# A fused eight-layer stack on one core: state-space inputs, small transfers and parameter work in another order

## The chip, the cores and the metric

The kernel runs on one core of a Trainium2 chip. The metric is the device time of one execution in microseconds (us); less is better. Five engines work side by side, each through its own stream in program order: PE (TensorE, matrix products), DVE (VectorE), ACT (ScalarE), POOL (GpSimd) and SP (SyncE, which only starts transfers here). ACT starts transfers too, in its own stream.

## What is computed

One sequence of 256 positions and width 2048 goes through two layers of a first block (a pooling mixer, dilated attention, each followed by a squared-ReLU MLP) and one layer of a second block, all in fp32. The change touches the mixer of the second block. Cut to it:

```
hn = rmsnorm(h, attn_norm_w);  proj = hn @ w_in            # 2048 -> 1024 + 512 + 256 + 64
u, c_q, c_kv, k_pe = split(proj)
# state-space group (S5): 64 groups of 16 inputs and 64 complex states
abar = exp(lam * dt);  zbar = (abar - 1) / lam;  bbar = zbar * b
s[t] = abar * s[t-1] + bbar @ u[t]                         # scan over 256 steps
y    = gelu(Re(c @ s) + d * u);  y_ssm = y * sigmoid(y @ w_glu + b_glu)
# latent attention (MLA), 8 heads, rotary on 64 of 192 dims, causal softmax
q = rmsnorm(c_q) @ w_uq;  k_nope, v = rmsnorm(c_kv) @ w_ukv
y_mla = softmax(mask(q k^T)) v
h = h + concat(rmsnorm(y_ssm), rmsnorm(y_mla)) @ w_out
```

A gated convolution MLP and a last norm follow.

## The kernel before

Activations lie as channel tiles of 128 channels by 256 positions. Every weight is streamed from HBM once, in units of 128 x 1024 elements (shorter ones in places). SP loads a unit (`raw`, `load_next`), ACT casts it to its high part (`hi`, L148), DVE subtracts for the low part (`lo`, L156), and PE makes three products, hi x hi, hi x lo and lo x hi (`mm3`, L206 to L208 in the second mixer, L211, L212 and L214 elsewhere). `take` keeps the high parts three units ahead of PE and the low parts three (two in the second mixer). A `slab` is a block of output columns over all input tiles. When its last product is issued, a generator (`on_done`) evacuates the accumulator and does what follows.

All other work is written as generators. After each weight unit `tick` runs one segment of every live generator (`step`) and takes one item of a background list (`pump`). So the code order, and with it each engine's stream, is set by how many `yield`s lie between two segments: one `yield` is one unit of PE work later.

**Parameters.** `ssm_params` (L888 to L1077) computes from the state-space parameters all that the mixer needs and stores it in HBM: `d_tab` (tables of powers of abar for the scan), `d_b` and `d_c` (128 x 512 and 128 x 768 blocks for each of eight groups of eight). It runs in the background of the first MLP, one segment for each unit. Its parts in order: loads of the parameters through ACT's stream (L897 to L905), an exponential (L907), a copy into `nat` (L908), three transposes on PE (L912), angle, magnitude and z on 128 x 32 tiles on DVE, complex products `cmul` (L923; six such tiny DVE operations each, all recorded on L921), the table on POOL (L988, L992), then for each of eight q: masked c (`cm`, POOL), b products (`pd` L1023, `bm` L1028, POOL), their transposes on PE (L1033, L1040), the pe/wl products (POOL) and final products (L1061).

**Second mixer.** `plan_mix2` lists the order of the weights, `run_mix2` uses them. w_in's first slab (four u tiles of 128 channels) starts before the norm's sums are ready (`raw`). Then come the c_q slab, the c_kv and k_pe slab, and the heads: projections of latents in two halves a = 0 and 1, and attention for two to four heads under them (`scores`, `soft`, `flip`, `attend`, `put`). The u tiles 4 and 5 are a slab under half a = 0, and 6 and 7 one under half a = 1. Then w_out's lower half on the MLA outputs (eight slabs), the GLU product (four slabs), and w_out's upper half on the state-space outputs.

**State-space steps.** For each of eight groups q, `ssm_step` does two half steps. The even one: products `bu` (L1184) from `us` and `qb`, and for the group two before (LAG = 2) `ssm_out`, products `y` (L1219). The odd one: `ssm_in` (DVE and POOL rotate bu), `ssm_mid` (scans and rotation back). `ssm_pace` lets a step go every second unit or so. Before a step, `u_done` (L1290) normalises a u tile (`ut`, POOL), stores it (`d_u`, L1301), and `load_u` loads it back as four transfers in another layout (`us`, L1157). `load_b`, `load_rec` and `load_c` (two transfers of 128 x 512, one of 128 x 512, two of 128 x 768) fetch that group's tables. After `y`, `gelu` copies y out of the accumulator (`yt`, L1227, ACT), stores it (`d_y`, L1228), loads it back as u (L1233) and applies Gelu (L1239). All of these transfers stand in ACT's stream. Statistics of the norms are sums on PE with a vector of ones (L334) over squares that POOL or ACT makes (`Sq`, L320 to L322).

A step asks for its input with these lines (before):

```
if not odd:
    if q < 8:
        if q not in us:
            if q in u_in:
                load_u(q)
            return False
        ssm_bu(q)
        if q < 7:
            load_b(q + 1)
```

Of the kernel before, what the change touches and what calls it, by code (L numbers as in the profile page):

```python
# [62 lines left out]
class Net:  # L63
# [824 lines left out]
    def ssm_params(self, sp):  # L888
# [53 lines left out]
        ni, zr, zi = a1[:, 1, :], z[:, 0, :], z[:, 1, :]  # L942
        tt(den, lr, lr, ALU.mult)
# [6 lines left out]
        tt(zr, zr, den, ALU.mult)  # L950
        tt(zi, ni, lr, ALU.mult)
# [20 lines left out]
        for n, a in ((2, a1), (1, a2), (0, a3)):  # L972
            cmul(e1, z, a)
            V.tensor_copy(zt[:, :, :, n], e1)
        for n, a in enumerate((a1, a2, a3, a4)):
            V.tensor_copy(at[:, :, :, n], a)
# [32 lines left out]
        for q in range(8):  # L1009
# [5 lines left out]
            wide = [P, 4, CH, 16]  # L1015
            for n in range(2):
                for a in range(2):
                    G.tensor_scalar(cm[:, n, a, :], cn[n][:, q, :], msk[:, 2 * n + a:2 * n + a + 1], None, op0=ALU.mult)
                prod = [sp.tile([P, 512], F32, tag=f"tmp{x}", name=f"pd{x}")[:, 0:256] for x in range(2)]
                prod = [x.rearrange("p (s l h) -> p s l h", s=4, l=CH) for x in prod]  # L1020
# [10 lines left out]
            pc = self.aux([P, 2, P])  # L1031
            for n in range(2):
                nc.tensor.transpose(pc[:, n, :], cm[:, n].rearrange("p a c -> p (a c)"), self.ident)  # L1033
            for n in range(2):
                nc.scalar.copy(wl[n][:, :, 0, :], pc[:, n, :].rearrange("p (s r) -> p s r", s=4))
            yield
            for n in range(2):
# [4 lines left out]
                yield  # L1042
# [36 lines left out]
    def plan_mix2(self):  # L1079
# [25 lines left out]
        for s in range(8):  # L1105
            self.want_slab(wo, 1024, 8, s * 256, nn=2)
# [669 lines left out]
```

## Time and profile before

| | |
|---|---|
| median of 3 runs | 3405.5 us (3404.15 to 3406.73) |
| profiled execution, its own time | 3404.18 us |
| span of its trace | 3402.4 us |
| mean granted PE clock | 0.977 of full |
| PE busy | 3277.6 us, 96% |
| DVE busy | 2142.9 us, 63% |
| ACT busy | 1606.5 us, 47% |
| POOL busy | 1233.2 us, 36% |

The table is read as follows. The span is the profiled execution from its first to its last instruction; busy is the time in which an engine worked on any instruction. The granted clock is a mean over the span: 1.00 is 2.4 GHz and 0.50 is 1.2 GHz. Lines L... are lines of the kernel before, unless a sentence says that they are of the changed one.

### The profile page before, as it was taken

The numbers are of one execution on the slowest core, as the hardware profiler recorded it, in microseconds if no ns is written. First come the engines' busy times: TensorE is split into PE (matmuls) and PEld (weight loads), VectorE is DVE, ScalarE is ACT, GpSimd is POOL, SyncE is SP. The second block draws the span as 40 slices with busy tenths as digits, with TensorE's granted clock in tenths as the row PEclk, the third lists the DMA queues.
The fourth block names the chain that finished last, engine by engine and source line by source line (L and its number), as shares of the span: only waits on it lengthen the run. The fifth ranks groups of instructions, "written<-read, shape, count | busy, mean of one in ns | idle before, by whom it ended". The sixth has DMA issues, their size and how long they took to land.

```text
span 3402.4 us, 49683 instructions
## 1 busy us (share of the span) xinstructions
PE 3277.6 (96%) x19452; PEld 2892.3 (85%) x19452; DVE 2142.9 (63%) x2748; ACT 1606.5 (47%) x2477; POOL 1233.2 (36%) x1371
## 2 busy tenths in 40 slices
PE   8998999999999999999999999996889999999999
PEld 7896888888898899988888888886879888888887
DVE  5777566665676545576565656674545686687585
ACT  4654444444554444465444444562346544444344
POOL 6454866662252000073121112454447332142141
PEclk9999999999999999999999999997789999999999
DMA  6555666666555554545555555544535555555554
GB/s 220 178 189 147 201 200 211 205 220 195 174 193 170 165 179 156 173 160 175 186 179 193 192 189 180 182 153 133 168 103 162 172 177 197 179 190 198 179 181 172
DMA packets 452165, 610.56 MB, mean 179 GB/s; under 512 B 56036, under 2 KB 262746, under 8 KB 451930
## 3 DMA queue, kind: packets, MB, share of 16 engines
q1 hardware_dynamic: 423914, 588.93, 53.0%
q10 hardware_dynamic: 27872, 17.87, 1.9%
q8 instruction: 152, 2.49, 0.3%
q14 instruction: 83, 0.68, 0.1%
q0 software_dynamic: 144, 0.59, 0.1%
HBM read 590.54 MB, written 16.78 MB: 178 GB/s over the span
## 4 chain that ended last, share of the span: by engine, by line
PE 80%; POOL 10%; DVE 4%; ACT 2%; issue 2%; DMA 1%; ACTq 1%; SPq 0%; POOLq 0%; DVEq 0%
PE acc L214 37%; PE acc L212 20%; PE acc L277 4%; PE acc L276 4%; PE acc L275 4%; PE acc L211 2%; PE acc L206 2%; PE acc L207 2%; PE acc L208 1%; DVE lo L156 1%; POOL w L629 1%; POOL X L441 1%; POOL tmp L988 1%; POOL hid L301 1%; PE y L1219 1%
## 5 line engine op out<-in xcount | busy, mean ns | idle before, releaser
L156 DVE TENSOR_TENSOR lo<-raw,hi 128x1024 fp32r<-128x1024 f32 x1094 | 1459.9, 1360 | 600.2 <-ACT hi L148 598.9
L214 PE MATMUL acc<-xs,hi 128*128 128x512 f32 x4020 | 1429.7, 397 | 9.5 <-POOL xs L445 9.4
L148 ACT CAST hi<-raw 128x1024 fp32r<-128x1024 f32 x1094 | 1118.9, 1045 | 574.5 <-PE acc L214 374.8
L212 PE MATMUL acc<-xs,lo 128*128 128x256 f32 x4288 | 1166.3, 282 | 8.6 <-DVE lo L156 8.6
L214 PEld LDWEIGHTS acc<-xs,hi 128*128 128x128 f32 x4020 | 761.1, 189 | 176.5 <-POOL xs L445 11.3
L212 PEld LDWEIGHTS acc<-xs,lo 128*128 128x128 f32 x4288 | 814.0, 190 | 32.8 <-DVE lo L156 10.1
L214 PE MATMUL acc<-hid,hi 128*128 128x512 f32 x1920 | 684.3, 396 | 0.0
L212 PE MATMUL acc<-hid,lo 128*128 128x256 f32 x2048 | 557.4, 282 | 3.4 <-DVE lo L156 3.4
L685 POOL TENSOR_TENSOR X<-X,c 128x256 f32<-128x256 f32 x152 | 134.3, 895 | 879.7 <-DVE X L683 566.1
L214 PEld LDWEIGHTS acc<-hid,hi 128*128 128x128 f32 x1920 | 361.5, 188 | 80.6
L212 PEld LDWEIGHTS acc<-hid,lo 128*128 128x128 f32 x2048 | 385.2, 188 | 16.4 <-DVE lo L156 4.0
L301 POOL TENSOR_TENSOR hid<-t,hid 128x256 fp32r<-128x256 f32 x128 | 147.1, 1173 | 447.6 <-ACT hid L300 445.1
L291 ACT COPY c<-acc 128x256 f32<-128x256 f32 x264 | 97.4, 373 | 305.4 <-PE acc L214 291.9
L206 PE MATMUL acc<-xs,hi 128*128 128x256 f32 (+1 forms) x768 | 223.6, 291 | 11.9 <-ACT t L287 5.6
L207 PE MATMUL acc<-xs,hi 128*128 128x256 f32 (+1 forms) x768 | 221.2, 288 | 1.1 <-DVE xs L447 0.6
L208 PE MATMUL acc<-xs,lo 128*128 128x256 f32 (+1 forms) x768 | 219.7, 286 | 0.6 <-DVE lo L156 0.6
L1624 POOL TENSOR_TENSOR a<-t,r 128x256 f32<-128x256 f32 x88 | 66.8, 761 | 369.9 <-DVE t L292 347.1
L292 DVE TENSOR_TENSOR t<-acc,c 128x256 f32<-128x256 f32 x208 | 87.5, 423 | 164.8 <-ACT c L291 162.3
L679 ACT COPY c<-acc 128x256 f32<-128x256 f32 x160 | 59.4, 373 | 219.2 <-PE acc L214 189.8
L206 PEld LDWEIGHTS acc<-xs,hi 128*128 128x128 f32 x768 | 149.7, 195 | 13.4 <-ACT t L287 6.2
L207 PEld LDWEIGHTS acc<-xs,hi 128*128 128x128 f32 x768 | 149.9, 195 | 1.9 <-DVE xs L447 0.8
L208 PEld LDWEIGHTS acc<-xs,lo 128*128 128x128 f32 x768 | 150.0, 195 | 1.0 <-DVE lo L156 1.0
(324 smaller groups left out, 4333.1 us busy)
## 6 DMA issues: line engine op xcount, KB each, us to landing
raw<-in_mlp_w_up_dram SPq DMA_DIRECT2D x128, 1024.0 KB
raw<-in_mlp_w_down_dram SPq DMA_DIRECT2D x128, 1024.0 KB
raw<-in_ffn_w_up_dram SPq DMA_DIRECT2D x176, 512.0 KB
raw<-in_attn_w_qkv_dram SPq DMA_DIRECT2D x96, 512.0 KB
raw<-in_ffn_w_down_dram SPq DMA_DIRECT2D x44, 1024.0 KB
raw<-in_attn_w_qkv_dram SPq DMA_DIRECT2D x24, 1024.0 KB
raw<-in_pool_w_in_dram SPq DMA_DIRECT2D x16, 1024.0 KB
raw<-in_pool_w_out_dram SPq DMA_DIRECT2D x16, 1024.0 KB
```

Source lines behind the costliest of these rows:

```text
L148: self.nc.scalar.copy(to(hi), src)
L156: self.nc.vector.tensor_tensor(out=to(lo), in0=src, in1=to(hi).bitcast(F32), op=ALU.subtract)
L206: nc.tensor.matmul(acc[:, 0:n], lhsT=hi, rhs=x[:, 0:n], start=first, stop=False)
L207: nc.tensor.matmul(acc[:, 0:n], lhsT=hi, rhs=x[:, n:2 * n], start=False, stop=False)
L208: nc.tensor.matmul(acc[:, 0:n], lhsT=lo, rhs=x[:, 0:n], start=False, stop=last)
L212: nc.tensor.matmul(acc[:, T:2 * T], lhsT=lo, rhs=x[:, 0:T], start=False, stop=False)
L214: nc.tensor.matmul(acc, lhsT=hi, rhs=x, start=False, stop=last)
L275: nc.tensor.matmul(a, lhsT=xh, rhs=hi[:, k, :], start=first and (t == 0 or not one), stop=False)
L276: nc.tensor.matmul(a, lhsT=xh, rhs=lo[:, k, :], start=False, stop=False)
L277: nc.tensor.matmul(a, lhsT=xl, rhs=hi[:, k, :], start=False, stop=last and (t == 1 or not one))
L301: (eng or nc.vector).tensor_tensor(out=xs[:, T:2 * T], in0=src, in1=xs[:, 0:T].bitcast(F32), op=ALU.subtract)
L685: (nc.vector if norm is not None and j >= KD - 2 else nc.gpsimd).tensor_tensor(out=x, in0=x, in1=c, op=ALU.add)
```

## The change

**Parameters.** Two segments more before the exponential and the copy into `nat`, three more before the transposes. The angle and z work is in five segments in place of two. One `cmul` runs in each segment; before, there were three, two, four, four and five (with the copies) in each. The table on POOL begins 18 units later (unit 29 of that stage against 11). In the loop over q, masked c and its transposes come first; the transposes of `bm` come one unit after its products for n = 1 and two for n = 0 (three before); the store into `d_b` comes two units later; two segments lie before the last products.

**Second mixer.** u tiles 4 and 5 are a slab directly behind the first one, so ahead of the c_q slab; u tiles 6 and 7 stay under half a = 1. `load_u` is now a generator in three segments, started from the even half step before: product on POOL, store, then the four loads. `load_rec(q)` comes right behind `bu` of q; `load_b` and `load_c` go to the odd half step. `gelu` stores y one segment behind the copy. Two of the eight w_out slabs on the MLA outputs go behind the GLU slabs; for that, the GLU output lies in tiles of its own instead of in `xs`.

```diff
         yield
+        yield
         nc.scalar.activation(ldt, ldt, AF.Exp)
         V.tensor_copy(nat[:, 2, :].rearrange("s (a p) -> s a p", a=2), ldt.to_broadcast([NS, 2, 64]))
-        yield
+        for _ in range(3):
+            yield
         ps = self.aux([P, 3, NS])
...
-        cmul(e2, e1, e1)
-        cmul(e3, e2, e1)
-        cmul(ep[:, 0], e2, e2)
-        yield
-        for n in range(1, NK):
-            cmul(ep[:, n], ep[:, n - 1], ep[:, n - 1])
-            if n % 2 == 0:
-                yield
-        cmul(a2, a1, a1)
-        cmul(a3, a2, a1)
-        cmul(a4, a2, a2)
-        yield
+        powers = [(e2, e1, e1), (e3, e2, e1), (ep[:, 0], e2, e2)]
+        powers += [(ep[:, n], ep[:, n - 1], ep[:, n - 1]) for n in range(1, NK)]
+        powers += [(a2, a1, a1), (a3, a2, a1), (a4, a2, a2)]
+        for w_ in powers:
+            cmul(*w_)
+            yield
...
                 yield
-            pc = self.aux([P, 2, P])
-            for n in range(2):
-                nc.tensor.transpose(pc[:, n, :], cm[:, n].rearrange("p a c -> p (a c)"), self.ident)
-            for n in range(2):
-                nc.scalar.copy(wl[n][:, :, 0, :], pc[:, n, :].rearrange("p (s r) -> p s r", s=4))
-            yield
-            for n in range(2):
+                if n == 0:
+                    yield
                 pb = self.aux([P, 4, P])
                 for s in range(4):
                     nc.tensor.transpose(pb[:, s, :], bm[n][:, s].rearrange("p l a h -> p (l a h)"), self.ident)
...
-        for c, nn in ((0, 4), (1024, 4), (1536, 2)):
+        for c, nn in ((0, 4), (512, 2), (1024, 4), (1536, 2)):
...
             def load_u(q):
-                us[q] = sp.tile([P, 4, NJ], F32, tag="us", name="us", bufs=3)
+
+                t = self.scr.tile([P, T], F32, tag="t", bufs=T_BUFS, name="ut")
+                tt(G, t.rearrange("p (l j) -> p l j", l=CH), lj(u[:, q, :]), lj(r1[0]), ALU.mult)
+                yield
+                load(out=self.d_u[q], in_=t)
+                yield
+                x = sp.tile([P, 4, NJ], F32, tag="us", name="us", bufs=3)
                 for l in range(CH):
-                    load(out=us[q][32 * l:32 * l + 32], in_=self.d_u[q][:, l * NJ:(l + 1) * NJ].rearrange("(s f) j -> f s j", s=4))
+                    load(out=x[32 * l:32 * l + 32], in_=self.d_u[q][:, l * NJ:(l + 1) * NJ].rearrange("(s f) j -> f s j", s=4))
+                us[q] = x
...
                         if q not in us:
                             if q in u_in:
-                                load_u(q)
+                                u_in.remove(q)
+                                self.start(load_u(q))
                             return False
                         ssm_bu(q)
-                        if q < 7:
-                            load_b(q + 1)
+                        if q:
+                            load_rec(q)
+                        if q + 1 in u_in:
+                            u_in.remove(q + 1)
+                            self.start(load_u(q + 1))
...
             self.slab(16, self.raw_x, u_done, raw=True)
+            self.slab(16, kx, u_done, n0=4, nn=2)
...
-            for s in range(8):
+            for s in range(6):
                 if s == 1:
                     self.start(self.rstd(s_mla, 1024, "r1", rm))
                 self.slab(8, from_heads, out_done(rm), n0=2 * s, nn=2)
...
+            for s in range(6, 8):
+                self.slab(8, from_heads, out_done(rm), n0=2 * s, nn=2)
```

**How the order moves, on DVE.** The place is the start of the powers in `ssm_params`, in the first MLP; L921 (L924 in the changed kernel) is one tiny operation of a `cmul`, `lo` is a weight unit's low part. Before:

```order
L156 TENSOR_TENSOR lo<-raw,hi 128x1024
L921 TENSOR_TENSOR wrk<-pw_2964 128x32 x2
L921 TENSOR_TENSOR pw_2965<-wrk 128x32
L921 TENSOR_TENSOR wrk<-pw_2964 128x32 x2
L921 TENSOR_TENSOR pw_2965<-wrk 128x32
L921 TENSOR_TENSOR wrk<-pw_2965,pw_2964 128x32 x2
L921 TENSOR_TENSOR pw_2966<-wrk 128x32
L921 TENSOR_TENSOR wrk<-pw_2965,pw_2964 128x32 x2
L921 TENSOR_TENSOR pw_2966<-wrk 128x32
L921 TENSOR_TENSOR wrk<-pw_2965 128x32 x2
L921 TENSOR_TENSOR ep<-wrk 128x32
```

In the changed kernel, from the same product on:

```order
L156 TENSOR_TENSOR lo<-raw,hi 128x1024
L924 TENSOR_TENSOR wrk<-pw_3050 128x32 x2
L924 TENSOR_TENSOR pw_3051<-wrk 128x32
L924 TENSOR_TENSOR wrk<-pw_3050 128x32 x2
L924 TENSOR_TENSOR pw_3051<-wrk 128x32
L156 TENSOR_TENSOR lo<-raw,hi 128x1024
L924 TENSOR_TENSOR wrk<-pw_3051,pw_3050 128x32 x2
L924 TENSOR_TENSOR pw_3052<-wrk 128x32
L924 TENSOR_TENSOR wrk<-pw_3051,pw_3050 128x32 x2
L924 TENSOR_TENSOR pw_3052<-wrk 128x32
L156 TENSOR_TENSOR lo<-raw,hi 128x1024
```

Between two low parts there stand six tiny operations now, where eighteen stood.

**On ACT.** The place is the first state-space groups, where the in-projection's slabs end (`us` is the input of `bu`, `qb` its table, `t` a slab's evacuation, L345 belongs to the norm's reciprocal root). Before:

```order
L148 CAST hi<-raw 128x4x128 x2
L1301 DMA d_u<-ut 128x256 x4
L345 ACT_TABLE_LOAD
L345 ACTIVATE m<-m,eps 128x2
L1157 DMA us<-d_u 32x4x64 x4
L148 CAST hi<-raw 128x4x128 x2
L287 COPY t<-acc 128x256 x2
L1162 DMA qb<-d_b 128x512 x2
L1166 DMA rec<-d_tab 128x512
L1157 DMA us<-d_u 32x4x64 x4
```

In the changed kernel:

```order
L1165 DMA d_u<-ut 128x256
L148 CAST hi<-raw 128x1024
L1169 DMA us<-d_u 32x4x64 x4
L1175 DMA qb<-d_b 128x512 x2
L148 CAST hi<-raw 128x1024
L287 COPY t<-acc 128x256 x2
L1165 DMA d_u<-ut 128x256
L148 CAST hi<-raw 128x1024
L287 COPY t<-acc 128x256 x2
L1169 DMA us<-d_u 32x4x64 x4
```

The four stores of one place are now one store for each group, two units ahead of its loads, and the loads of the second group come behind two evacuations of the slab that PE finishes directly ahead of `bu`. On PE the first sum with the ones vector behind the first slab (L334) follows 96 of the stage's products now, directly behind the moved u slab; before it followed 144 of the c_q slab's.

## Rows read from the trace of the kernel before

**Rows 1.** Windows: us, PE, PEld, DVE, ACT, POOL busy (instructions), PE clock, DMA share, GB/s
```profile
282.00:320.00 38.00, 32.37 (x161) 27.28 (x161) 34.29 (x138) 15.18 (x26) 8.52 (x19) 0.90 0.42 137
...
450.00:850.00 400.00, 398.06 (x2373) 344.80 (x2372) 249.05 (x248) 184.34 (x276) 220.58 (x202) 1.00 0.64 205
...
2281.70:2517.30 235.60, 186.24 (x1162) 173.70 (x1163) 114.86 (x220) 81.00 (x178) 92.42 (x110) 0.78 0.44 129
```

**Rows 2.** Waits of PE, 265 to 325 us: us in total, times, longest us
```profile
PE aux L912 <- DVE nat L908: 6.5, 1, 6.5
...
PE acc L211 <- DVE t L292: 2.9, 1, 2.9
...
PE acc L212 <- DVE lo L156: 2.9, 1, 2.9
```

**Rows 3.** Timeline of ACT, 266 to 283 us: start, us, instruction, idle before
```profile
269.69 5.35 ACTq L903 DMA_DIRECT2D bn<-in_ssm_b_im_dram  x1
...
278.33 1.04 ACT L148 CAST hi<-raw 128x1024 fp32r<-128x1024 f32 x1 [8.04 <-issue]
```

**Rows 4.** Groups of DVE, 286 to 320 us: xcount, busy us, mean ns, idle before
```profile
L156 DVE TENSOR_TENSOR lo<-raw,hi 128x1024 fp32r<-128x1024 f32 x8 | 9.7, 1218 | 0.8 <-ACT hi L148 0.8
...
L921 DVE TENSOR_TENSOR wrk<-pw,pw 128x32 f32<-128x32 f32 x20 | 3.6, 220 | 0.2
```

**Rows 5.** Waits of PE, 325 to 800 us
```profile
PE aux L1061 <- POOL wl L1055: 1.9, 4, 0.5
...
PE aux L1040 <- POOL bm L1028: 0.7, 1, 0.7
```

**Rows 6.** Groups of POOL, 330 to 460 us
```profile
L988 POOL TENSOR_TENSOR tmp<-wt,ep 128x256 f32<-128x256 f32 (+5 forms) x40 | 27.4, 705 | 1.2
...
L1028 POOL TENSOR_TENSOR bm<-pd,pd 64x256 f32<-64x256 f32 x6 | 8.1, 1348 | 0.3
...
L1023 POOL TENSOR_TENSOR pd<-bn,zt 128x256 f32<-128x256 f32 x8 | 6.1, 785 | 0.0
```

**Rows 7.** Waits of PE, 2275 to 2520 us
```profile
PE bu L1184 <- DMA us<-d_u: 20.4, 4, 8.1
...
PE aux L334 <- POOL Sq L322: 11.0, 2, 6.8
...
PE acc L206 <- ACT t L287: 9.6, 1, 9.6
...
PE y L1219 <- POOL st L1120: 8.8, 3, 6.8
```

**Rows 8.** Timeline of ACT, 2302 to 2450 us: DMA issues
```profile
2303.30 0.33 ACTq L1301 DMA_DIRECT2D d_u<-ut  x1
...
2306.98 1.79 ACTq L1157 DMA_DIRECT2D us<-d_u  x4
...
2332.77 1.89 ACTq L1157 DMA_DIRECT2D us<-d_u  x4
...
2409.81 1.89 ACTq L1157 DMA_DIRECT2D us<-d_u  x4
```

**Rows 9.** Timeline of PE, 2310 to 2415 us: two of a slab, then two bu
```profile
2310.36 0.28 PE L208 MATMUL acc<-xs,lo 128*128 128x256 f32 x1
...
2310.48 0.28 PE L206 MATMUL acc<-xs,hi 128*128 128x256 f32 x1
...
2339.90 3.65 PE L1184 MATMUL bu<-us,qb 128*128 128x64 f32 x16 [8.15 <-DMA us<-d_u]
...
2414.24 3.65 PE L1184 MATMUL bu<-us,qb 128*128 128x64 f32 x16 [4.09 <-DMA us<-d_u]
```

**Rows 10.** Waits of ACT, 2275 to 2520 us
```profile
ACT yt L1227 <- PE y L1219: 40.1, 6, 12.4
...
ACT hi L148 <- DMA rec<-d_tab: 11.4, 1, 11.4
```

**Rows 11.** Waits of PE, 2520 to 2720 us
```profile
PE acc L206 <- ACT t L287: 5.6, 3, 3.5
```

More of the change, by code (lines that the diff above doesn't have):

```diff
@@ L950, in ssm_params @@
         tt(zr, zr, den, ALU.mult)
+        yield
         tt(zi, ni, lr, ALU.mult)
@@ L1015, in ssm_params @@
             wide = [P, 4, CH, 16]
+            prod = [sp.tile([P, 512], F32, tag=f"tmp{m}", name=f"pd{m}") for m in range(2)]
+            prod = [x[:, 0:256].rearrange("p (s l h) -> p s l h", s=4, l=CH) for x in prod]
             for n in range(2):
@@ L1018, in ssm_params @@
                     G.tensor_scalar(cm[:, n, a, :], cn[n][:, q, :], msk[:, 2 * n + a:2 * n + a + 1], None, op0=ALU.mult)
-                prod = [sp.tile([P, 512], F32, tag=f"tmp{x}", name=f"pd{x}")[:, 0:256] for x in range(2)]
-                prod = [x.rearrange("p (s l h) -> p s l h", s=4, l=CH) for x in prod]
+                yield
+            pc = self.aux([P, 2, P])
+            for n in range(2):
+                nc.tensor.transpose(pc[:, n, :], cm[:, n].rearrange("p a c -> p (a c)"), self.ident)
+            for n in range(2):
+                nc.scalar.copy(wl[n][:, :, 0, :], pc[:, n, :].rearrange("p (s r) -> p s r", s=4))
+            for n in range(2):
                 G.memset(bm[n], 0.0)
@@ L1041, in ssm_params @@
                 nc.scalar.copy(o[:, :, n, :], pb)
-                yield
-            nc.sync.dma_start(out=self.d_b[q], in_=o.rearrange("p s n c -> p (s n c)"))
             wide = [P, 4, CH, 32]
@@ L1052, in ssm_params @@
                 if n == 0:
+                    nc.sync.dma_start(out=self.d_b[q], in_=o.rearrange("p s n c -> p (s n c)"))
                     G.tensor_tensor(out=wl[0][:, :, 1:, :], in0=tm[0], in1=tm[1], op=ALU.add)
@@ L1056, in ssm_params @@
                 yield
-            yield
+            for _ in range(2):
+                yield
             pd = self.aux([P, P])
@@ L1227, in gelu @@
                 nc.scalar.copy(yt, y)
+                yield
                 load(out=self.d_y[q], in_=yt)
-                for _ in range(2):
-                    yield
+                yield
                 uq = u[:, q, :]
@@ L1283, in ssm_step @@
                     if q < 7:
-                        load_rec(q + 1)
-                    if q + 1 in u_in:
-                        load_u(q + 1)
+                        load_b(q + 1)
+                    if 0 <= q - LAG + 1 < 8:
+                        load_c(q - LAG + 1)
                 self.n_ssm += 1
@@ L1297, in u_done @@
                     yield
-                t = self.scr.tile([P, T], F32, tag="t", bufs=T_BUFS, name="ut")
-                tt(G, t.rearrange("p (l j) -> p l j", l=CH), lj(u[:, j, :]), lj(r1[0]), ALU.mult)
-                yield
-                load(out=self.d_u[j], in_=t)
                 u_in.append(j)
@@ L1495, in run_mix2 @@
                     self.pump = both
-                    self.slab(16, kx, u_done, n0=4 + 2 * a, nn=2)
+                    self.slab(16, kx, u_done, n0=6, nn=2)
                     self.pump = pump
-                if a == 1:
                     free.append(a)
@@ L1526, in from_heads @@
                 return xs[:, 8 + k, :]
-            for s in range(8):
+            for s in range(6):
                 if s == 1:
@@ L1556, in run_mix2 @@
                 self.slab(8, from_ys, glu_done, n0=2 * s, nn=2)
+            for s in range(6, 8):
+                self.slab(8, from_heads, out_done(rm), n0=2 * s, nn=2)
             def from_yo(k):
```

16 lines of the change are left out of this document (10 added, 6 removed).

## The prediction, made before the changed kernel ran

> **What bounds the kernel now.** I read first the windows by stage. In a dense stretch of the MLP PE is busy for 398.06 of 400 us at full clock [rows 1]: there only less PE work could help, and the change removes none. So the change can win only where PE falls idle or runs at half clock, and the windows show two such places that it touches: the start of the parameter work (282 to 320 us) and the second mixer from its first statistics to the out product (2281.7 to 2517.3 us). Next I read what PE waited for in both. In the first it waits for DVE three times, 6.5, 2.9 and 2.9 us [rows 2]; in the second for transfers of `us`, for the squares `Sq`, for an evacuation on ACT and for `st` [rows 7]. Last I read the timelines and groups of the engines that it waited for.
>
> **Parameters: what goes.** Two transfer issues hold ACT: one takes 5.35 us, and the next cast of a high part starts 8.04 us late [rows 3]. `nat` (L908) waits behind them, and the transposes (L912), in PE's stream, wait 6.5 us for `nat` [rows 2], although weight units were ready. A unit is 16 matmuls, and a dense matmul takes 400/2373 = 0.169 us [rows 1], so 2.7 us. Putting the transposes three units later moves them by 8.1 us, more than the 6.5; the three units of look-ahead cover ACT's 8 us. That wait goes: -6.5.
>
> Then the powers. One `cmul` is six operations of about 0.2 us, 1.3 us at most; a low part is 1.2 us [rows 4]. With three or four of the products per unit DVE needs 5 to 6.5 us for a unit of 2.7 us; with one it needs 2.5. From 282 to 320 us PE did 161 matmuls, worth 161 x 0.169 = 27.1 us, in 38: 10.9 us are lost, in the two waits of 2.9 and in matmuls at half clock (granted 0.90) [rows 1, 2]. Evacuations come on top of 2.5 us in some units, so the margin is thin, but it is an average and the look-ahead carries it. I take all 10.9; the bound on the other side is 0 to 3 us left over. Together -17.4 (-17.4 to -14).
>
> **Parameters: what comes.** The transposes of `bm` stand one unit (2.7 us) behind two `pd` and two `bm` operations on POOL for n = 1, 2 x 0.785 + 2 x 1.348 = 4.3 us [rows 6]. Where POOL isn't ahead of PE this is a wait of 1.6 us, eight times: +13. Where it is ahead, nothing: below 0 I see no reason. The nearest rows are the waits of the same kind before, 0.4 to 0.7 us each, five times [rows 5]; eight of these are +3, and I take that. Table building on POOL (forty L988 alone are 27.4 us [rows 6]) only moves by 18 units within the same MLP: 0, with 3 either way, since PE depends on POOL there through the hidden tiles. Parameters: -14.4 (-17 to 0).
>
> **Second mixer: the price of a wait.** PE is busy for 186.24 of 235.6 us, 49.4 idle, at a mean clock of 0.78 [rows 1]. 0.78 = 1 - 0.44/2, so 104 us run at 1.2 GHz; if the idle time lies in them, 54 us of work ran at half rate, and 27 us of these are surplus. Each us of wait has cost 27/49.4 = 0.55 us more. I count waits, and multiply by 1.55.
>
> **Waits on `us`: 20.4 before [rows 7].** Now each group issues its four loads in the unit just ahead of its `bu`. The issues take 1.79 to 1.89 us [rows 8], so two of them end at 2334.66 and 2411.70; `bu` started 2339.90 - 2334.66 = 5.24 us and 2414.24 - 2411.70 = 2.54 us after that [rows 8, 9]. That is 4.3 to 7.1 us for a load with nothing under it. By group, read from where the loads stand in ACT's order and `bu` in PE's: q0 has most of a slab under it, 0 to 4.3, I take 2; q1 stands behind the evacuations of the slab that PE finishes right ahead of `bu`, q2 behind the root of the statistics, 5.7 each; q3 is hidden, 0; q4 and q5 have 24 products of 0.12 us (2310.48 - 2310.36 [rows 9]) = 2.9 us under them, 2.8 each; q6 has its store directly ahead, and from store to loads it took 3.7 us [rows 8], so 8.0 to 10.8, 9.4; q7 2.8. The sum is 31 (21 to 42): +10.8 (0 to +21). Queued behind them on ACT are the high parts and `yt`; PE is ahead of neither by more than the look-ahead, so they come into the same wait.
>
> The Trainium skill (DMA: Bandwidth & Descriptors, section Anatomy of one DMA) puts the fixed part of a transfer at about 2.0 us. The rows show 2.5 and 5.2, and the measurement decides. By 2.0 the eight waits would be some 19 us, and the whole time some 3372, an estimate.
>
> **Other waits.** The 9.6 us on an evacuation [rows 7] come from `rec`: its load in ACT's stream waits for a buffer and holds a high part for 11.4 us [rows 10]. Behind `bu` of the same group it asks later, when the older scan is done: -9.6 (-9.6 to -4). Of the 11.0 us on `Sq` the longest, 6.8, follows four `ut` products put on POOL together; they come one by one now, and I leave 3.8: -3 (-6.8 to 0). `st`: 8.8 before; the y products still follow the same chain of scans two groups behind: -0.8 (-4 to +4). ACT's largest wait, 40.1 us for `yt` on y [rows 10], stays in the order, ahead of high parts. Waits: +10.8 - 9.6 - 3 - 0.8 = -2.6, times 1.55 = -4.
>
> **The shift of the first sum.** It follows 96 products where 144 stood, so 48 x 0.12 = 5.8 us less work covers DVE's norm of the input; DVE has two low parts (1.2 each [rows 4]) less ahead of it: +3.5 (0 to +5.8). Reordering the GLU and out product slabs, and the new tiles for the GLU output: 0. PE's largest wait there, 5.6 us [rows 11], belongs to slabs that don't move; should the moved slabs uncover one like it, +6. The later store of y and the loads of tables at odd steps: 0, hidden behind two groups of lag; if not, they are in the bound of `st`.
>
> **Sum.** -14.4 - 4 + 3.5 = -14.9 us on the profiled execution's 3404.18 (span 3402.4 and 1.8 around it): 3389.3. The median of the runs, 3405.5, is 1.3 above that execution: 3390.6, so **3391**.
>
> **Rivals.**
> (a) The mixer gains as well. If the loads are mostly under other work (21 us of waits), and the `Sq` wait goes whole, waits change by +0.6 - 9.6 - 6.8 - 0.8 = -16.6, times 1.55 = -26; with +3.5 - 14.4 and 1.3 that is 3369. For it: each `ut`, store and load starts one group earlier by the code. Against: the order above puts the loads' issue directly ahead of `bu`. Chance 0.26; with no wait on `us` left for most groups it would go to some 3355.
> (b) Slower: every group waits for its own loads. Eight times 7.1 us [rows 8, 9] is 57, +36.4 over before; the waits change by +36.4 - 9.6 - 3 - 0.8 = +23, times 1.55 = +36, and +3.5 - 14.4 + 1.3 makes 3431. It decides from a sum of `us` waits of about 45 us, where the loss passes the gain of the parameters by 0.2%. For it: 7.1 was seen, and ACT's evacuations stand ahead of the issue. Against: four of eight groups have products under their loads. Chance 0.15. The Trainium skill (DMA: Bandwidth & Descriptors, Rules for kernel authors) asks to issue a transfer early, compute, and wait late; this change does the opposite for q1 and q2, and the trace's 4.09 and 8.15 us agree with the rule.
> (c) The parameters' gain is given back on POOL: +13 in place of +3 gives 3401. For it: the one-unit distance. Against: POOL was late by 0.7 us at most. Chance 0.13.
> My forecast keeps 0.46.
>
> **How the numbers follow.** About 0.2%, 6.8 us, is what a measurement of this kernel can tell from no change; faster means below 3398.7, slower above 3412.3. Faster: 0.32 of the forecast, all 0.26 of (a), 0.01 of (c): 0.59. Same: 0.13 of the forecast, 0.10 of (c): 0.23. Slower: 0.15 of (b), 0.01 of the forecast, 0.02 of (c): 0.18. The forecast's own range is 3376 to 3407. The range takes in (a) down to 3362 and the lower part of (b) up to 3416.
>
> **What would show it.** In the parameters: no wait of PE at the three transposes, the stretch from 270 to 320 us as dense as the rest of the MLP, at clock 1.00, and waits at the transposes of `bm` of some 3 us in all. In the mixer: no wait on the evacuation by `rec`; waits of `bu` on `us` near 31 us, the longest at q6; first statistics to out product near 236 us, since the 3.5 us and the waits cancel. The prediction is wrong if the waits on `us` are below 20 or above 45 us, if the stretch's clock leaves 0.78 by more than 0.05, or if DVE is still late for PE after 282 us.

## The result, and the profile after

The changed kernel is slower: median 3426.73 us (3421.84 to 3430.82) beside 3406.11 us for the kernel before on the same chip, a ratio of 1.0061 (95% interval 1.0043 to 1.0078), 20.6 us more. The profiled execution took 3427.84 us, its span is 3426.1. Medians here and below are over runs in the fast state, which leaves out one run of e15_tables (6422.72 us).

| | before | after |
|---|---|---|
| PE busy | 3277.6 us | 3301.4 us |
| DVE / ACT / POOL busy | 2142.9 / 1606.5 / 1233.2 us | 2138.5 / 1609.2 / 1238.4 us |
| mean granted PE clock | 0.977 | 0.970 |
| first statistics of the mixer to the out product | 235.6 us | 261.3 us |
| from the out product to the end | 885.1 us | 882.3 us |

PE has as many instructions as before (19452) and is busy 23.8 us longer: it did the same products slower. One event of fixed work tells where. The last statistics of the first block start at 2235.16 us before and at 2234.86 us after: so up to there the whole parameter part is worth 0.3 us in these two profiles. Everything lost is behind it.

Windows of the changed kernel (length, PE, PEld, DVE, ACT and POOL busy with instructions, PE clock, DMA share, GB/s): the start of the parameter work, then the mixer up to the first scores of the heads, then the heads.

```profile
282.00:325.00 43.00, 43.00 (x248) 37.44 (x247) 37.34 (x94) 24.84 (x40) 8.93 (x9) 1.00 0.66 218
2282.50:2424.00 141.50, 112.18 (x716) 110.55 (x716) 66.31 (x112) 42.00 (x72) 52.39 (x56) 0.76 0.45 128
2424.00:2543.80 119.80, 96.88 (x498) 82.95 (x497) 50.87 (x109) 44.17 (x110) 41.15 (x54) 0.69 0.33 102
```

The last two together, from the first sum with the ones vector to the out product:

```profile
2282.50:2543.80 261.30, 209.06 (x1211) 193.51 (x1211) 117.19 (x221) 86.18 (x182) 93.54 (x110) 0.73 0.39 116
```

The same two stretches of the mixer before:

```profile
2281.70:2391.10 109.40, 82.09 (x587) 81.22 (x588) 59.76 (x99) 36.37 (x66) 47.40 (x50) 0.81 0.46 134
2391.10:2517.30 126.20, 104.15 (x577) 92.48 (x577) 55.09 (x121) 44.62 (x112) 45.01 (x61) 0.75 0.42 124
```

The first row answers to the 282 to 320 us of [rows 1]: no idle time at all and clock 1.00. The other rows say what went wrong. Up to the first scores PE did 129 instructions more than before and the stretch took 32.1 us more; in the heads it did 79 fewer and the stretch took only 6.4 us less. Idle time is nearly the same, 27.3 + 22.1 = 49.4 us before and 29.3 + 22.9 = 52.2 us after. The clock is what fell, 0.81 to 0.76 and 0.75 to 0.69.

Which instructions moved is read from the same windows by tile (PE's busy us, and instructions in brackets; one across an edge counts on both sides):

| | before: to the first scores | before: heads | after: to the first scores | after: heads |
|---|---|---|---|---|
| products on `xs` (in-projection) | 46.12 (336) | 13.42 (96) | 53.73 (385) | 11.56 (96) |
| `bu` | 9.69 (64) | 11.17 (64) | 20.53 (96) | 5.62 (32) |
| `y` | 8.17 (48) | 26.63 (144) | 20.98 (96) | 19.45 (96) |
| scores `sc` | 0.05 (1) | 24.68 (96) | 0.03 (1) | 29.30 (96) |

The heads have as many products on `xs` as before. The slab of u tiles 4 and 5, "under half a = 0" by the code, already stood ahead of the first scores before, where PE did its 96 products at full clock:

```profile
2376.80:2391.10 14.30, 11.54 (x96) 11.33 (x96) 0.00 (x0) 0.00 (x0) 0.00 (x0) 1.00 0.71 215
```

What moved is 48 products from ahead of the first sum, and two of the eight state-space steps from the heads: `bu` of groups 4 and 5 (32 instructions) and with it `y` of groups 2 and 3 (48). Groups 4 and 5 need u tiles 4 and 5, which are there earlier now.

PE's waits of the changed kernel in the parameter part; the first answers to L1040 and the second to L1033 of the kernel before:

```profile
PE aux L1044 <- POOL bm L1037: 10.0, 4, 4.9
PE aux L1026 <- POOL cm L1022: 4.2, 3, 1.9
```

Its waits in the mixer, which answer to [rows 7]:

```profile
PE bu L1197 <- DMA us<-d_u: 13.7, 5, 5.6
PE bu L1197 <- DMA raw<-in_mla_w_uq_dram: 9.8, 1, 9.8
PE bu L1197 <- DMA rec<-d_tab: 8.2, 1, 8.2
PE y L1232 <- DMA qc<-d_c: 7.0, 2, 4.7
PE aux L334 <- POOL Sq L322: 5.1, 1, 5.1
...
PE bu L1197 <- DMA qb<-d_b: 0.5, 1, 0.5
PE acc L206 <- ACT t L287: 0.3, 1, 0.3
```

Among the lines left out is one more at `y`:

```profile
PE y L1232 <- POOL st L1126: 2.0, 1, 2.0
```

The wait on an evacuation behind `rec`, 9.6 us before, is 0.3 us. All waits at `bu` are 13.7 + 9.8 + 8.2 + 0.5 = 32.2 us. `y` now waits for its table `qc`, which no row showed before. The 8.2 us are a wait for `us`, whatever their name: they are in front of q6, and its last load of `us` landed at 2458.85.

```profile
2458.95 3.65 PE L1197 MATMUL bu<-us,qb 128*128 128x64 f32 x16 [8.18 <-DMA rec<-d_tab]
```

### The profile page after: what moved, and what is told of

Read it like the earlier page. It is cut to its first block, busy times and chain, and to the rows that moved or that the text cites. A ratio compares the mean times of both kernels' runs of the same rounds, so it can differ in the third digit from the quotient of the medians.

```text
span 3426.1 us, 49678 instructions
## 1 busy us (share of the span) xinstructions
PE 3301.4 (96%) x19452; PEld 2914.8 (85%) x19452; DVE 2138.5 (62%) x2748; ACT 1609.2 (47%) x2479; POOL 1238.4 (36%) x1371
## 4 chain that ended last, share of the span: by engine, by line
PE 82%; POOL 8%; DVE 4%; issue 2%; DMA 2%; ACT 2%; ACTq 1%; SPq 0%; POOLq 0%; DVEq 0%
PE acc L214 38%; PE acc L212 21%; PE acc L277 4%; PE acc L276 4%; PE acc L275 4%; PE acc L211 2%; PE acc L206 2%; PE acc L207 2%; PE acc L208 2%; DVE lo L156 1%; PE y L1232 1%; POOL w L629 1%; POOL X L441 1%; POOL hid L301 1%; PE bu L1197 1%
## 5 line engine op out<-in xcount | busy, mean ns | idle before, releaser
L156 DVE TENSOR_TENSOR lo<-raw,hi 128x1024 fp32r<-128x1024 f32 (+1 forms) x1094 | 1460.7, 1361 | 622.2 <-ACT hi L148 620.9
L148 ACT CAST hi<-raw 128x1024 fp32r<-128x1024 f32 (+1 forms) x1094 | 1118.7, 1045 | 600.1 <-PE acc L214 394.8
L214 PEld LDWEIGHTS acc<-xs,hi 128*128 128x128 f32 x4020 | 762.5, 190 | 177.1 <-POOL xs L445 11.3
L212 PEld LDWEIGHTS acc<-xs,lo 128*128 128x128 f32 x4288 | 815.8, 190 | 28.8 <-DVE lo L156 6.7
L301 POOL TENSOR_TENSOR hid<-t,hid 128x256 fp32r<-128x256 f32 x128 | 145.6, 1163 | 447.1 <-ACT hid L300 444.9
L207 PE MATMUL acc<-xs,hi 128*128 128x256 f32 (+1 forms) x640 | 187.9, 294 | 8.0 <-DVE xs L447 8.0
L206 PE MATMUL acc<-xs,hi 128*128 128x256 f32 (+1 forms) x640 | 189.3, 296 | 5.9 <-DVE X L683 4.7
L208 PE MATMUL acc<-xs,lo 128*128 128x256 f32 (+1 forms) x640 | 186.2, 291 | 0.0
L207 PEld LDWEIGHTS acc<-xs,hi 128*128 128x128 f32 x640 | 128.0, 200 | 9.6 <-DVE xs L447 9.5
L206 PEld LDWEIGHTS acc<-xs,hi 128*128 128x128 f32 x640 | 128.2, 200 | 6.7 <-DVE X L683 5.0
L277 PE MATMUL acc<-hi,hid 128*128 128x512 f32 x328 | 130.9, 399 | 0.0
```

The source lines that it names most:

```text
L148: self.nc.scalar.copy(to(hi), src)
L156: self.nc.vector.tensor_tensor(out=to(lo), in0=src, in1=to(hi).bitcast(F32), op=ALU.subtract)
L206: nc.tensor.matmul(acc[:, 0:n], lhsT=hi, rhs=x[:, 0:n], start=first, stop=False)
L207: nc.tensor.matmul(acc[:, 0:n], lhsT=hi, rhs=x[:, n:2 * n], start=False, stop=False)
L208: nc.tensor.matmul(acc[:, 0:n], lhsT=lo, rhs=x[:, 0:n], start=False, stop=last)
L212: nc.tensor.matmul(acc[:, T:2 * T], lhsT=lo, rhs=x[:, 0:T], start=False, stop=False)
```

## The experiments

Each kernel is timed beside the kernel before on the same chip; the ratio is to it, with its 95% interval. The groups ran on different chips, where the kernel before took 3406.0 to 3408.6 us, so a difference of medians across groups is good to some 3 us. `e11_us` to `e15_tables` and `e18_tables_us` stand on the part of the change that had proved good.

| kernel | median, us | ratio |
|---|---|---|
| e1_params | 3401.5 | 0.9985 (0.9975 to 0.9994) |
| e2_mix | 3429.2 | 1.0065 (1.0050 to 1.0080) |
| e3_front | 3389.1 | 0.9946 (0.9931 to 0.9961) |
| e4_outorder | 3406.8 | 1.0000 (0.9990 to 1.0009) |
| e5_slab | 3430.6 | 1.0075 (1.0057 to 1.0093) |
| e6_steps | 3425.1 | 1.0056 (1.0037 to 1.0075) |
| e7_early | 3416.3 | 1.0028 (1.0018 to 1.0038) |
| e8_tables | 3422.8 | 1.0045 (1.0029 to 1.0061) |
| e9_fill | 3419.0 | 1.0035 (1.0022 to 1.0047) |
| e10_bm | 3386.2 | 0.9949 (0.9933 to 0.9964) |
| e11_us | 3368.7 | 0.9893 (0.9878 to 0.9908) |
| e12_rec | 3375.9 | 0.9912 (0.9897 to 0.9927) |
| e13_both | 3380.0 | 0.9920 (0.9904 to 0.9936) |
| e14_slab | 3402.9 | 0.9984 (0.9974 to 0.9993) |
| e15_tables | 3372.9 | 0.9898 (0.9880 to 0.9915) |
| e16_slab_kept | 3395.8 | 0.9968 (0.9955 to 0.9981) |
| e17_slab_back | 3368.4 | 0.9885 (0.9869 to 0.9902) |
| e18_tables_us | 3364.4 | 0.9876 (0.9861 to 0.9891) |

### Which half, and which part of the parameters

**e1_params**: all hunks of the diff up to `plan_mix2`, the mixer as before.

> The kernel before with the parameter part of the change alone. Theory: the three waits at the start (6.5, 2.9, 2.9 us) and the half clock around them go, some 17 us, and PE then waits about as long for bm and cm on POOL, because the transposes stand one or two units behind their products: 3403 to 3406 us, waits at the transposes of bm and cm some 14 us in all. Rival: the start's gain stays and all the loss of the change lies in the mixer: 3389 to 3393 us.

**e2_mix**: the hunks from `plan_mix2` on, the parameters as before.

> The kernel before with the mixer part of the change alone (u slab, loads, steps and slab order). Theory: the whole loss of the change is here: 3424 to 3434 us. Rival: the mixer loses less and part of the loss comes from the parameter part, by what it shifts later: 3410 to 3420 us.

**e3_front**: the parameter hunks without the loop over q.

> The kernel before with the parameter part up to the powers and z alone (later transposes, one complex product per unit); the loop over q is that of before. Theory: the 17 us of waits and half clock go and nothing comes back: 3388 to 3394 us, waits for bm and cm as before, about 3 us. Rival: what is late comes back whatever the loop does, since the table building falls 18 units later on POOL beside the loop: 3400 to 3406 us.

Measured: 3401.5, 3429.2 and 3389.1 us. The mixer holds the whole loss: alone it costs 1.0065, the whole change 1.0061. The start of the parameter part gains 0.54%, some 18 us; the loop over q gives 3401.5 - 3389.1 = 12.4 us of it back. e1_params lies just under the range of its theory, with the waits at the transposes that it named (9.7 and 4.2 us). What PE waits for there is seen on POOL in the changed kernel (start, us, instruction, idle before), and then on PE:

```profile
660.97 1.56 POOL L301 TENSOR_TENSOR hid<-t,hid 128x256 fp32r<-128x256 f32 x2 [12.22 <-ACT hid L300]
662.48 0.52 POOL L1030 MEMSET bm<- 128x512 f32 x1
662.96 2.23 POOL L1032 TENSOR_TENSOR pd<-bn,zt 128x256 f32<-128x256 f32 x2
665.16 2.38 POOL L301 TENSOR_TENSOR hid<-t,hid 128x256 fp32r<-128x256 f32 x2
667.50 1.51 POOL L1037 TENSOR_TENSOR bm<-pd,pd 64x256 f32<-64x256 f32 x2
```

```profile
669.06 1.12 PE L1044 MATMUL aux<-ident,bm 128*128 128x128 f32 x4 [4.90 <-POOL bm L1037]
```

POOL works in order, and operations of the MLP stand in its stream (L301, `hid`). It had finished the products of n = 0 at 648.7 us and then stood 12.22 us in front of a `hid` whose input ACT had not made. Only at 662.48 could it begin `bm` of n = 1, with another `hid` in the middle, and the transposes one unit later waited 4.90 us. So this wait, the longest, is set by when the main loop lets POOL go on, not by the 4.3 us of POOL work.

**e10_bm**: all of the parameter part, transposes three units behind their products.

```diff
-                if n == 0:
+                for _ in range(2):
                     yield
...
-            for _ in range(2):
-                yield
+            yield
             pd = self.aux([P, P])
```

> The parameter part of the change alone, with the transposes of bm three units behind their products for both n, as far as before. Theory: the waits at the transposes of bm (9.7 us in the parameter part alone) go and the gain of the start stays: 3387 to 3394 us. Rival: it was the clock or the other order of the loop: 3398 to 3404 us.

Measured: 3386.2 us. The waits at L1044 fall from 10.0 to 1.3 us, and the whole gain of the start stays:

```profile
PE aux L1026 <- POOL cm L1022: 2.2, 2, 1.6
PE aux L1044 <- POOL bm L1037: 1.3, 1, 1.3
```

### Which part of the mixer

**e4_outorder**: only the two w_out slabs behind the GLU slabs, with the new tiles.

```diff
-            for s in range(8):
+            for s in range(6):
...
+            for s in range(6, 8):
+                self.slab(8, from_heads, out_done(rm), n0=2 * s, nn=2)
```

> The kernel before with the slab order of the out product alone (two of eight slabs behind the GLU slabs, GLU output in tiles of its own). Theory: the stretch behind the heads got 3.3 us shorter in the changed kernel by this: 3402 to 3404 us. Rival: that came from the steps' own time, the order does nothing: 3405 to 3407 us.

Measured: no difference, within 0.1%. The rival holds; the order of these slabs does nothing by itself.

**e5_slab**: only the place of the u slab.

```diff
-        for c, nn in ((0, 4), (1024, 4), (1536, 2)):
+        for c, nn in ((0, 4), (512, 2), (1024, 4), (1536, 2)):
...
             self.slab(16, self.raw_x, u_done, raw=True)
+            self.slab(16, kx, u_done, n0=4, nn=2)
...
-                if a < 2:
+                if a == 1:
```

> The kernel before with the u slab of columns 512 to 768 moved ahead of the c_q slab alone; steps and loads as before. Theory A (the slab was cover): PE reaches the first sum 6 to 7 us late for the same work, and half a = 0 of the heads has 96 products less to put under waits and chains: 3414 to 3422 us. Theory B (late loads): the slab's place costs no more than those 6 us, and u tiles that are there earlier give some back: 3403 to 3412 us.

**e6_steps**: only `load_u` as a generator, the other half steps of the table loads, and the later store of y.

> The kernel before with the loads and steps of the change alone (product, store and loads of u one group ahead, table loads in the other half step, y stored a segment later); the slab stays under the heads. Theory B: this is the loss, since every group waits for its own loads on ACT and PE runs the stretch at half clock longer: 3422 to 3432 us, PE waits at bu of 30 us or more. Theory A: without the slab's move the loads cost less than half of the 21 us: 3408 to 3416 us.

Measured: 3430.6 and 3425.1 us, each about as much as both together (3429.2). For the slab, theory A's range was too low by 9 us. For the loads, theory B's range held, and so did its waits at `bu` (24.9 us named `us` and 5.4 named `rec`). Both cost, and they do not add. The windows of e5_slab, up to the first scores and in the heads:

```profile
2287.10:2434.80 147.70, 107.79 (x717) 106.59 (x715) 65.04 (x112) 42.97 (x74) 54.05 (x58) 0.76 0.43 125
2434.80:2545.90 111.10, 94.29 (x498) 81.02 (x497) 51.21 (x108) 41.79 (x106) 41.21 (x52) 0.74 0.36 107
```

The heads are 15.1 us shorter than before (126.2), the stretch up to them 38.3 us longer (109.4), with 39.9 us idle in place of 27.3. And of e6_steps, where no product moved across the first sum:

```profile
2286.30:2408.10 121.80, 96.08 (x627) 94.78 (x627) 67.68 (x110) 38.16 (x69) 51.02 (x56) 0.78 0.46 130
2408.10:2542.30 134.20, 106.51 (x537) 91.38 (x537) 49.25 (x109) 42.74 (x108) 39.00 (x54) 0.70 0.36 108
```

Together they are 256.0 us with as many instructions as before (1164), where before took 235.6. Idle time is 53.4 us in place of 49.4; PE's busy time is 202.6 in place of 186.2. So the late loads cost little idle time, and 16 us by the same work done slower.

**e7_early**: the mixer part, with u stored as soon as it is normalised (the lines of `u_done` before), and its loads issued in the even half step.

```diff
                     if 0 <= q - LAG < 8:
                         ssm_out(q - LAG)
+                    if q + 1 in u_in:
+                        u_in.remove(q + 1)
+                        load_u(q + 1)
```

> The mixer part of the change, with product and store of u as before (as soon as the u tile is normalised) and the four loads of the next group issued right behind bu and y, half a step earlier than before. Theory B: the waits at bu on us go below 10 us, and with them most of the loss: 3402 to 3412 us. Theory A: what is lost is the cover, the waits move to another releaser: 3418 to 3428 us.

Measured: 3416.3 us, 13 of the 21 us of the mixer part back, a little under theory A's range and above B's. The waits at `bu` named `us` fall to 4.7 us, as B has it, but 9.3 us on an evacuation come in, as A has it. The lateness of u is real, and not all.

**e8_tables**: the mixer part with the table loads in their former half steps.

```diff
-                        if q:
-                            load_rec(q)
+                        if q < 7:
+                            load_b(q + 1)
...
+                    if 0 <= q - LAG + 1 < 8:
+                        load_c(q - LAG + 1)
                 else:
...
-                    if q < 7:
-                        load_b(q + 1)
-                    if 0 <= q - LAG + 1 < 8:
-                        load_c(q - LAG + 1)
+                    if q < 7:
+                        load_rec(q + 1)
```

> The mixer part of the change, with the table loads (qb, qc, rec) where they were before. If the table loads in the odd half step delay bu (the 9.8 us and 8.2 us waits of the changed kernel ended with transfers other than us): 3416 to 3422 us. If not, as the mixer part alone: 3426 to 3432 us; if the table loads were a gain of the change (the 9.6 us wait behind rec comes back): 3434 to 3440 us.

Measured: 3422.8 us, 6 us less than e2_mix, just above the first range; the intervals of the two ratios (1.0029 to 1.0061 and 1.0050 to 1.0080) overlap, so the 6 us are not clear of noise. The row at `bu` that names a weight (`raw`) is explained by ACT's stream in the changed kernel:

```profile
2398.53 1.77 ACTq L1169 DMA_DIRECT2D us<-d_u  x4
2400.40 6.69 ACTq L1246 DMA_DIRECT2D u<-d_y  x4
2407.13 1.64 ACTq L1175 DMA_DIRECT2D qb<-d_b  x2
...
2409.94 1.04 ACT L148 CAST hi<-raw 128x1024 fp32r<-128x1024 f32 x1 [11.05 <-DMA qb<-d_b]
```

From the first of four loads of u (`d_y`) to the end of the last it took 6.69 us, where others took 1.8; `qb` stood behind them, was issued until 2408.77 us, and `bu` of q5 started at 2410.43. Little of the 6.69 us is issuing. Here are the loads one by one as far as the rows part them, and a weight load on SP:

```profile
2400.40 0.39 ACTq L1246 DMA_DIRECT2D u<-d_y  x1
2405.19 0.79 ACTq L1246 DMA_DIRECT2D u<-d_y  x2
2406.02 1.07 ACTq L1246 DMA_DIRECT2D u<-d_y  x1
...
2399.60 0.37 SPq L138 DMA_DIRECT2D raw<-in_w_in_dram  x1
```

Between the first and the second there are 4.40 us. In the trace the second waits for semaphore 103, the counter that is to mark its own landing; SP's load of 1 MB is marked by the same one. That load landed at 2405.17, and 0.02 us later ACT went on. The second load of `qb` likewise waited for semaphore 101 and a weight load on it (landed 2408.40, issued 2408.42), which is why the wait at `bu` carries a weight's name. In e2_mix, the same program in the mixer, it is named by `qb`:

```profile
PE bu L1193 <- DMA us<-d_u: 13.8, 5, 5.3
PE bu L1193 <- DMA qb<-d_b: 9.5, 1, 9.5
```

The first group shows what ACT's order does to everything behind it:

```profile
2298.76 1.82 ACTq L1169 DMA_DIRECT2D us<-d_u  x4
2305.05 2.05 ACTq L1175 DMA_DIRECT2D qb<-d_b  x2
2307.14 1.04 ACT L148 CAST hi<-raw 128x1024 fp32r<-128x1024 f32 x1 [10.69 <-PE bu L1197]
```

The loads of `us` wait for their own store (landed at 2298.74 us), `qb` for `bu` (it shares its buffers with the group before), and a high part stands 10.69 us behind them.

**e9_fill**: extra products in front of five `bu`. They only fill PE; nothing reads what they write.

```diff
                 bus[q] = bu_p.tile([P, 2, T], F32, tag="bu", name="bu")
+                for k in range({0: 12, 1: 24, 2: 16, 5: 40, 6: 36}.get(q, 0)):
+                    nc.tensor.matmul(bus[q][:, k % 2, 0:P], lhsT=self.ident, rhs=self.ident, start=True, stop=True)
```

> The changed kernel with 128 extra products that nothing reads (identity by identity, 128x128), put in front of bu of groups 0, 1, 2, 5 and 6, where PE waits 2.8 to 9.8 us; 12, 24, 16, 40 and 36 of them, sized to fit into those waits. Theory (the loss is half clock on work behind the waits, not more waiting): PE's granted clock from first sum to out product rises from 0.73 to 0.78 or more and the time falls to 3412 to 3422 us. Rival (the waits themselves are the loss): the clock may rise, the time stays or rises by the part that does not fit: 3425 to 3436 us.

The stretch, and in it the extra products alone:

```profile
2279.10:2537.90 258.80, 231.97 (x1468) 214.92 (x1467) 118.62 (x221) 86.41 (x182) 95.01 (x110) 0.78 0.40 118
...
2279.10:2537.90 258.80, 29.47 (x256) 29.00 (x256) 0.78 0.40 118
```

Measured: 3419.0 us, within the range of the theory, and clock 0.78 in the stretch. But the profile bears the theory out in small part only: the stretch took 258.8 us, 2.5 less than 261.3, and most of that execution's difference in time lies ahead of it. The 128 products (256 instructions) took 29.5 us, of which 25.4 came out of idle time (52.2 to 26.8 us). The others took 202.5 us in place of 209.1, some 6.6 us less, which fits the higher clock, and the fill that didn't fit into waits took 4.1 of it. The ratios are 1.0035 (1.0022 to 1.0047) and 1.0061 (1.0043 to 1.0078); the profiled execution, 3422.85 us, is among the longer of its nine. Inconclusive on what the clock is worth.

### What of the change is worth keeping

These stand on e3_front (3389.1 us).

**e11_us**: before's mixer with only the diff of e7_early's `load_u` above; **e12_rec**: only the load of `rec` behind its own group's `bu`; **e13_both**: both.

```diff
                         if q < 7:
                             load_b(q + 1)
+                        if q:
+                            load_rec(q)
...
-                    if q < 7:
-                        load_rec(q + 1)
```

> The kernel before with the parameter part up to the powers (3389 us) and one step of the mixer: the four loads of the next u issued right behind bu and y, half a step earlier than before, where u is there. If the waits at bu on us (20.4 us before) go with it: 3370 to 3384 us. If they only move to another releaser: 3386 to 3394 us.

> The kernel before with the parameter part up to the powers (3389 us) and one step of the mixer: the load of rec for a group right behind its bu, as in the change, not one half step earlier. If the 9.6 us wait behind rec's buffer goes and nothing comes: 3372 to 3382 us. If rec then lands late for the rotation and delays the chain: 3386 to 3396 us.

> The kernel before with the parameter part up to the powers, the u loads half a step earlier and the rec load behind bu of its own group. If the two gains (20 and 13 us) stand in different waits they add: 3353 to 3362 us, with the 8.6 us wait behind ACT's evacuation and most of the us waits gone. If ACT's order makes one of the other: 3364 to 3372 us.

Measured: 3368.7, 3375.9 and 3380.0 us. Each alone gains what was expected, e11_us a little more. Together they are worse than e11_us and no better than e12_rec, outside both ranges that were expected. PE's waits in e11_us:

```profile
PE y L1221 <- POOL st L1122: 10.7, 5, 7.1
PE acc L206 <- ACT t L287: 8.6, 1, 8.6
PE bu L1186 <- DMA us<-d_u: 7.2, 3, 4.1
```

and in e13_both:

```profile
PE y L1221 <- POOL st L1122: 19.3, 8, 7.1
...
PE bu L1186 <- DMA us<-d_u: 8.8, 3, 6.1
...
PE acc L206 <- ACT t L287: 0.4, 1, 0.4
```

The wait behind ACT's evacuation goes (8.6 to 0.4 us), and `y` waits 19.3 us for `st` in place of 10.7. `rec` now lands too late for the rotation ahead of the scans. In e13_both DVE waits for it, and in e11_us no wait of DVE names it:

```profile
DVE vp L1122 <- DMA rec<-d_tab: 19.4, 2, 11.9
```

e12_rec has this wait too, 22.1 us, and gains all the same; what makes the two gains one was not tried apart.

**e14_slab**: e11_us with the slab moved as in e5_slab.

> The kernel with the u loads half a step earlier (3369 us), and the u slab of columns 512 to 768 moved ahead of the c_q slab. If the slab's place costs by itself, as cover that half a = 0 of the heads loses and as work that stands where DVE's norm is late: 3386 to 3396 us. If the slab only cost because u's loads came late behind it: 3368 to 3378 us.

Measured: 3402.9 us, 34 more than e11_us (31 by the ratios), above the range of the first case. The slab's place costs by itself.

**e15_tables**: e13_both with `qb` and `qc` in the odd half step; **e18_tables_us**: e11_us with the same. The calls are the ones that e8_tables moves, the other way; `rec` stays.

> The kernel of e13_both with the loads of qb and qc in the odd half step, as in the change. If these loads are late there, since qb shares its two buffers with the group before and lands just ahead of bu: 5 to 12 us above e13_both, with PE waits at bu or y that end with qb or qc. If not: within 4 us of it.

> The kernel with the u loads half a step earlier (3369 us) with the loads of qb and qc in the odd half step, as in the change, rec as before. If they are late there: 3374 to 3384 us; if the shorter issue ahead of y helps: 3358 to 3365 us.

Measured: 3372.9 (7 less than e13_both) and 3364.4 us (4 less than e11_us, in the second range). No case of e15_tables had foreseen a gain. With u early this part of the change may help a little, and with u late (e8_tables) it may cost; in all three the intervals of the ratios overlap, so none is clear of noise alone.

**e16_slab_kept**: the changed kernel with e10_bm's and e7_early's edits; **e17_slab_back**: the same with the slab back under the heads.

> The changed kernel with two things mended: transposes of bm three units behind their products, and u stored as soon as it is normalised with its loads right behind bu and y. The parts add up if this takes 3395 to 3405 us (3427 less 12 to 16 for bm and less 12 for u). If u's lateness was the whole of the mixer's loss: 3376 to 3390 us.

> The same with the u slab of columns 512 to 768 back under half a = 0 of the heads. Theory (the heads take as long with or without it, so ahead of them it costs its own time and more): 20 to 34 us less than e16_slab_kept, 3366 to 3380 us. Rival (its place doesn't matter once u is early): within 6 us of it.

Measured: 3395.8 and 3368.4 us: 27.4 us for the slab's place. The two stretches, up to the first scores and the heads, in e16_slab_kept:

```profile
2267.10:2395.40 128.30, 106.45 (x716) 104.49 (x715) 66.82 (x112) 43.10 (x74) 55.22 (x58) 0.79 0.48 140
2395.40:2514.50 119.10, 97.89 (x497) 83.48 (x497) 49.93 (x109) 42.64 (x107) 42.95 (x52) 0.72 0.35 104
```

and in e17_slab_back:

```profile
2265.20:2355.30 90.10, 78.10 (x587) 77.07 (x588) 60.70 (x99) 36.95 (x67) 47.13 (x51) 0.89 0.58 169
2355.30:2483.10 127.80, 106.24 (x578) 93.46 (x577) 54.38 (x121) 44.01 (x112) 45.16 (x59) 0.75 0.39 119
```

With the slab ahead, the stretch up to the first scores is 38.2 us longer for 129 instructions more, and the heads are only 8.7 us shorter for 81 fewer. By tile these are the instructions counted above for the changed kernel: 48 products from ahead of the first sum, and `bu` and `y` of two steps. The slab's own 96 products stand ahead of the first scores in both. So the theory of e17_slab_back, that the heads take as long with the slab as without, has the right time and the wrong reason: the slab was never under the heads' scores. The two steps that leave the heads shorten them by 8.4 us of PE's time (106.24 to 97.89) and hardly any idle time; ahead of the heads PE takes 28.4 us for the 129 instructions, at clock 0.79 beside 0.89, and is idle for 21.9 us in place of 12.0.

e18_tables_us has the lowest median, 1.24% (1.09% to 1.39%) under the kernel before; the intervals of e11_us and e17_slab_back overlap its own.

## Why the prediction was wrong

On the two profiled executions, with 48 products at 0.12 us = 5.8 us counted as work that moved behind the first sum:

| term | forecast, us | measured, us |
|---|---|---|
| parameters | -14.4 | -0.3 |
| lateness of the first sum | +3.5 | +6.9 |
| waits of the mixer and their price | -4 | +19.9 |
| from the out product on | 0 | -2.8 |
| sum | -14.9 | +23.7 |

The step that failed most is the third term: the waits came near, and their price did not. It failed with either edit of the mixer alone: with the late loads (e6_steps) for the same instructions, and with the moved slab (e5_slab), which the prediction had only in the second term.

- **Start of the parameters, -17.4: right.** e3_front measured about -18, and the window at 282 us is dense at clock 1.00. By the diff the exponential comes one segment later and the transposes three in all, as the sum has it.
- **Transposes of `bm`, +3: the size failed.** I took eight waits like the nearest rows [rows 5] and named +13 as the bound, which is rival (c); 12.4 was measured. Those rows came from a distance of three units. The wait is made by the `hid` operations in POOL's stream, which I named for the table and left out here: POOL can't run ahead of the main loop past them. With this, the parameter part by itself gains 0.15%, some 5 us, not 14.
- **Waits on `us`, 31 us: near in sum, 32.2, in part by luck.** Waits for `us` are 13.7 + 8.2 = 21.9 us; q0, q1, q3 and q6 came within 1.2 us of their forecasts. The longest, 10.4 at q5 where I had 2.8, ends with `qb` behind other loads on ACT, a load that I had put at 0. The evacuation's wait behind `rec` went, as forecast. Waits for `Sq` were 5.1, forecast 8. Waits of `y` were 9.0, forecast 8, but 7.0 of them end with `qc`, also put at 0.
- **The sum of the waits, -2.6: near,** idle time rose by 2.9 us. But rival (b), which names the sign that came, isn't what happened either: its price was 57 us of waits on `us`.
- **The price of a wait, 1.55: failed.** It took the half clock as a fixed part of the waits. With nearly the same idle time the clock went from 0.78 to 0.73, and PE's busy time in the stretch rose from 186.24 to 209.06 us. Of these 22.8 us, 5.8 are work that moved into the stretch; 17 us are the same work done slower. By tile, `bu` took 5.3 us more for the same instructions, `y` 5.6 and the scores 4.6. In e6_steps 4.0 us more of idle time came with 16.4 us more of busy time, where the price of 1.55 has 2.2.
- **The moved slab, +3.5: failed; alone it costs as much as the whole change.** I priced only that DVE's norm had less work to hide behind. The runs show 25 us (e5_slab), 31 to 34 (e14_slab) and 27 (e16_slab_kept less e17_slab_back) for its place. PE reached the first sum 1.1 us later with 48 products less done, so 6.9 us for the term I gave 3.5, above the bound of 5.8. The rest, which I had nowhere in the sum, is that two steps come ahead of the heads with the slab's tiles, and that the slab's dense products no longer stand ahead of group 4. That PE takes longer for the steps there is shown; how much of it is the missing slab and how much the loads that they wait for is open, and so is why the clock fell.
- **Out product and GLU order, 0: right** (e4_outorder).

That the slab and the late loads each take some 20 us and both together no more is shown; which of the two would have to give way in each wait was not traced.

## What to carry to other kernels

Before work is moved, ask which later steps its result makes ready, and what will stand between them: here a slab took two steps with it, and their place cost more than its own. A producer that shares an in-order engine with work of the main loop can't run ahead of it, so the distance to its consumer is counted in turns of that loop, not in its own durations. Where PE's idle time is scattered, don't price the lower clock as a fixed share of it: read busy time for the same products. And when transfers that usually issue in 1.8 us take 6.7, look at them one by one and at the semaphores that they wait for.

## What the runs showed of the hardware that was not expected

A load on ACT's stream stood for 4.40 us, and the work behind it with it, because a 1 MB load that SP had issued used the same semaphore and had not landed. 128 extra products in front of waiting ones left the stretch's length nearly as it was (258.8 and 261.3 us), while its clock rose from 0.73 to 0.78 and the other products took some 6.6 us less.
